# One queue in source order for the transfers of the first three products of an encoder block

## Chip, cores and metric

The kernel runs on one core of a Trainium2 chip. The metric is the device time of one execution in microseconds (us). PE is TensorE, DVE VectorE, ACT ScalarE, POOL GpSimd, SP the engine that issues most transfers.

## What is computed

One encoder block for 256 tokens `x` and 256 memory tokens `mem` of width 2048, all in float32. Cut to what matters here:

```python
h = rms_norm(x, g_mix);  proj = h @ w_in          # q, k, v of mixers A, B; q of C; three gates
mkv = rms_norm(mem, g_mem) @ w_mem_kv             # k and v of mixer C: the first two products
kc = rms_norm(split_heads(mkv[..., :C_W]), g_kc)  # each head normed again with its gains
# A: dilated windows with a bias; B: grouped queries with rotary; C: cross-attention into mem
x = x + (sum of gates * branch @ w_br) @ w_o
hf = rms_norm(x, g_ffn) @ w_ffn_in
x = x + (silu(hf[..., :D_FF]) * hf[..., D_FF:]) @ w_ffn_out
```

The row scale of an RMS norm (one number for each token) is applied behind the product, and the gains `g` in front of it, on the transposed tokens.

## The kernel before, in words

**A product.** `product` (line 150) multiplies 256 tokens by a weight of 2048 x 512 (4.19 MB): 16 blocks k of 128 rows. A block has six matmuls of 128x128 by 128x512: for each half t of the tokens, high x high, high x low and low x high (lines 172 to 174), since every operand is split into a high and a low part in TensorE's float32r. The two halves go to two PSUM banks from a pool of four (`pmm`), so every second product writes the same banks again and needs them evacuated.

**Splits.** `split` (line 72) makes the high part on ACT (line 75, or 78 with gains) and the remainder on DVE (76, 79). Weights go from `raw` (three buffers, two blocks of 512 KB in each load of the first two products, four blocks in the third) to `whi` and `wlo` (four buffers of two blocks). `load_T` (179) does the same for the transposed tokens, 256 KB for two blocks: its `get(k)` issues the transfer to `rawT` (two buffers) on ACT's queue (190) when block k is first asked for, and splits it right after.

**Order.** The first three products are `w_mem[0]` (keys of mem), `w_mem[1]` (values of mem) and `w_qkv[0]`. Beside them generators run as side jobs: `product` calls `tick` (129) after each block, and a tick advances at most one job whose pause, counted in blocks, is over. `row_sums` (198) loads 512 KB of token rows on SP, pauses, squares them on ACT with a running sum (206), four times, and then makes the row scale on DVE. `take_slots` (289) evacuates a product: squares of the banks (298), a pause, a wait for the row scale, the head scale `hf` (309), a pause, then the scaled copy `y` out of the banks (313), the gains and the rotary on POOL, the transposes of heads `hT` on PE. `constants` (241) loads head gains `gh`, the rotary table and a bias table on SP; `fetch` (249) asks for the blocks of xT ahead.

This order in the source isn't the order on the engines. The program is handed to a planner, which simulates the engines and their transfers and picks, for each engine, among the instructions that are ready in its simulation the one that is earliest in the source. The order that it finds is fixed: on the chip each engine runs its list in order and waits at an instruction whose data has not come. `s4` tiles (rows, `y`, squares, rotary) share five buffers of 4 KB in each partition.

Of the kernel before, what the change touches and what calls it, by code (L numbers as in the profile page):

```python
# [11 lines left out]
F32 = mybir.dt.float32  # L12
F32R = mybir.dt.float32r
I32 = mybir.dt.int32
AF = mybir.ActivationFunctionType
# [3 lines left out]
P = 128  # L19
S = 256  # L20
T = S // P
D = 2048
KT = D // P
HD = 128
DFF = 5632
NC = 512
KF = DFF // P
PK, LOAD = 2, 4
# [8 lines left out]
BUCKETS, MAX_DIST = 32, 1024  # L37
# [13 lines left out]
def encoder_block(ctx: ExitStack, tc: tile.TileContext, a: dict, out: bass.AP):  # L51
    nc = tc.nc
    const = ctx.enter_context(tc.tile_pool(name="const", bufs=1))
    wp = ctx.enter_context(tc.tile_pool(name="wp", bufs=3))
    big = ctx.enter_context(tc.tile_pool(name="big", bufs=11))
    mid = ctx.enter_context(tc.tile_pool(name="mid", bufs=5))
    small = ctx.enter_context(tc.tile_pool(name="small", bufs=4))
    dram = ctx.enter_context(tc.tile_pool(name="dram", bufs=1, space=bass.MemoryType.DRAM))
    pmm = ctx.enter_context(tc.tile_pool(name="pmm", bufs=4, space=bass.MemoryType.PSUM))
# [2 lines left out]
    def s8(shape, name, dt=F32R, pool=None):  # L62
        return (pool or big).tile(shape, dt, name=name, tag="s8")

    def s4(shape, name, dt=F32):
        return mid.tile(shape, dt, name=name, tag="s4")

    def at_bank(name):
        return pat.tile([P, NC], F32, name=name, tag="at")


    def split(hi, lo, src, scale=None):

        if scale is None:
            nc.scalar.activation(hi, src, AF.Copy)  # L75
            nc.vector.tensor_sub(lo, src, hi.bitcast(F32))  # L76
        else:
            nc.scalar.activation(hi, src, AF.Copy, scale=scale)
            nc.vector.scalar_tensor_tensor(lo, src, scale, hi.bitcast(F32), op0=ALU.mult, op1=ALU.subtract)
# [22 lines left out]
    def row_scale(ss, r):  # L102

        v = small.tile([P, T], F32, name="rs_v")
        nc.vector.tensor_scalar(v, ss, 1.0 / D, EPS, op0=ALU.mult, op1=ALU.add)
        y = rsqrt(v, [P, T], nc.vector)
        nc.vector.tensor_copy(r[:, 0], y)
        nc.vector.tensor_mul(r[:, 1], y, y)


    side, now = [], [0]

    def advance(job):

        try:
            lag = next(job[1])
            job[0] = now[0] + (lag or 1)
            return lag is not None
        except StopIteration:
            side.remove(job)  # L120
            return True

    def start(steps):

        job = [0, steps]
        side.append(job)
        advance(job)

    def tick():
        now[0] += 1  # L130
        for job in list(side):
            if job[0] <= now[0] and advance(job):
                break
# [5 lines left out]
    def load(src, k0, nk):  # L139

        raw = wp.tile([P, LOAD, NC], F32, name="raw")
        if nk % PK:
            c = k0 % PK * NC
            nc.sync.dma_start(out=raw[:, 0], in_=src[k0 // PK][:, c:c + NC])
        else:
            nc.sync.dma_start(out=raw[:, :nk].rearrange("p (u k) n -> p u (k n)", k=PK),
                              in_=src[k0 // PK:(k0 + nk) // PK].rearrange("u p n -> p u n"))
        return raw

    def product(src, lhs, nk, head=(), beside={}):  # L150


        ps = [pmm.tile([P, NC], F32, name="mm") for _ in range(T)]
        k0 = 0
        while k0 < nk:
            n = head[0] if head else min(LOAD, nk - k0)
            head = head[1:]
            if k0 in beside:
                start(beside[k0])
            lhs(k0)  # L160
            raw = load(src, k0, n)
            for b in range(0, n, PK):
                m = min(PK, n - b)
                hi = wp.tile([P, PK, NC], F32R, name="whi", bufs=4)
                lo = wp.tile([P, PK, NC], F32R, name="wlo", bufs=4)
                split(hi[:, :m], lo[:, :m], raw[:, b:b + m])
                for i in range(m):
                    k = k0 + b + i
                    xh, xl = lhs(k)
                    for t in range(T):  # L170
                        c = slice(t * P, (t + 1) * P)
                        nc.tensor.matmul(ps[t], lhsT=xh[:, c], rhs=hi[:, i], start=(k == 0), stop=False)  # L172
                        nc.tensor.matmul(ps[t], lhsT=xh[:, c], rhs=lo[:, i], start=False, stop=False)  # L173
                        nc.tensor.matmul(ps[t], lhsT=xl[:, c], rhs=hi[:, i], start=False, stop=(k == nk - 1))  # L174
                    tick()
            k0 += n
        return ps

    def load_T(src, g, tag):

        tiles = [s8([P, 4, 2, S], tag) for _ in range(KT // 4)]
        have = set()

        def get(k):
            k0 = k // 2 * 2
            tl = tiles[k // 4]
            if k0 not in have:
                have.add(k0)
                raw = wp.tile([P, 2, S], F32, name="rawT", bufs=2)
                nc.scalar.dma_start(out=raw, in_=src[k0 // 2].rearrange("p (k s) -> p k s", s=S))  # L190
                for i in range(k0, k0 + 2):
                    split(tl[:, i % 4, 0], tl[:, i % 4, 1], raw[:, i - k0], g[:, i:i + 1])
            return tl[:, k % 4, 0], tl[:, k % 4, 1]
        return get

# [2 lines left out]
    def row_sums(src, r, pace, name):  # L198

        ss = small.tile([P, T, 2], F32, name="rss", bufs=1)  # L200
        for t in range(T):
            for h in range(2):
                rows = s4([P, D // 2], "rows")
                nc.sync.dma_start(out=rows, in_=src[t * P:(t + 1) * P, h * (D // 2):(h + 1) * (D // 2)])
                yield pace
                nc.scalar.activation(rows, rows, AF.Square, accum_out=ss[:, t, h:h + 1])  # L206
        sr = small.tile([P, T], F32, name="ss", bufs=1)
        nc.vector.tensor_reduce(sr, ss, axis=AX.X, op=ALU.add)
        row_scale(sr, r)
        known.add(name)  # L210

    def transposed(src, dst, g=None):

        for h in range(2):
            tp = at_bank("tp")
            for k in range(2):
                for t in range(T):
                    nc.tensor.transpose(tp[:, k * S + t * P:k * S + (t + 1) * P],  # L218
                                        src[t][:, (2 * h + k) * P:(2 * h + k + 1) * P], ident)
            if g is None:  # L220
                d = dst(2 * h, 2)
                split(d[0], d[1], tp.rearrange("p (k s) -> p k s", s=S))
            else:
                for k in range(2):
                    d = dst(2 * h + k, 1)
                    split(d[0], d[1], tp[:, k * S:(k + 1) * S], g(2 * h + k))
# [10 lines left out]
    gh = const.tile([P, 6, HD], F32, name="gh")  # L237
    rope = const.tile([P, 2, T, HD // 2], F32, name="rope")
    relb = const.tile([P, A_HEADS], F32, name="relb")

    def constants():
        v = a["g_heads"]
        nc.sync.dma_start(out=gh, in_=bass.AP(tensor=v.tensor, offset=v.offset, ap=[[0, P], [HD, 6], [1, HD]]))
        yield 1
        nc.sync.dma_start(out=rope, in_=a["rope"])
        nc.vector.memset(relb[:64], NEG)
        nc.sync.dma_start(out=relb[:BUCKETS], in_=a["rel_bias"])

    def fetch(get, pace):
        for k in range(0, KT, 2):  # L250
            get(k)
            yield pace
# [174 lines left out]
    r_m, r_x, r_f = (scales[:, i] for i in range(3))  # L427
    memT = load_T(a["memT"], gT[:, 1], "memT")
    xT = load_T(a["xT"], gT[:, 0], "xT")
    memT(0)  # L430
    first = product(a["w_mem"][0], memT, KT, (1, 1) + (2,) * 7, {6: row_sums(a["mem"], r_m, 3, "mem")})
    start(constants())
    start(take_slots(first, MEM_SLOTS[:4], r_m, "mem", nc.vector))
    start(fetch(xT, 2))
    start(take_slots(product(a["w_mem"][1], memT, KT, (2,) * 8), MEM_SLOTS[4:], r_m, "mem"))
    oT = [s8([P, 4, 2, S], f"oT{i}") for i in range(3)]
    ol = lambda k: (oT[k // 4][:, k % 4, 0], oT[k // 4][:, k % 4, 1])
    for c in range(8):
        sums = {} if c else {0: row_sums(a["x"], r_x, 3, "x")}
        start(take_slots(product(a["w_qkv"][c], xT, KT, beside=sums), SLOTS[4 * c:4 * c + 4], r_x))  # L440
        if c == 0:
            start(biases())
# [28 lines left out]
    x = [s8([P, D], f"x{t}", F32) for t in range(T)]  # L471
# [20 lines left out]
    for c0, c1 in ((0, 6), (6, KF // 4)):  # L492
        hT = []
        for n in range(c0, c1):
            ap = product(a["w_ffn_a"][n], x1l, KT)
# [7 lines left out]
            tl = s8([P, 2, 4, S], "hT", pool=tail if n % 6 < 4 and n < 6 or n > 8 else None)  # L503
# [91 lines left out]
```

## Time and profile before

| | us |
|---|---|
| median of 3 runs | 1437.49 (1437.03 to 1438.25) |
| profiled run, its own time | 1438.22 |
| its span | 1436.4 |
| PE busy | 1416.7 (99%) |
| DVE busy | 781.2 (54%) |
| ACT busy | 667.2 (46%) |
| POOL busy | 78.8 (5%) |
| transfers, mean | 193 GB/s |

How to read it: a busy PE is not PE at its peak, since matmuls overlap; what one matmul costs is seen in the distance between two starts. TensorE's clock has two levels, 1.2 and 2.4 GHz, shown as a granted share of 0.5 or 1.0. In rows of time the first number is the start in us from the start of the span, the second the duration; brackets hold the idle time of the engine before the instruction and what ended it. ACTq and SPq are issues of transfers by these engines.

### The profile page before, as it was taken

To read this page: it belongs to the slowest core of one execution; us is meant where nothing else is said; L and a number is where in the kernel's file an instruction comes from. 1 tells how busy PE (TensorE), PEld (TensorE's weight loads), DVE (VectorE), ACT (ScalarE), POOL (GpSimd) and SP (SyncE) were. 2 spreads that over 40 slices of the span, in tenths; PEclk is the share of its full clock that TensorE was granted. 3 is DMA by queue.
4 is the path that set the end of the run, shared out by engine and by line. 5 is a ranking of instruction groups with operands and counts; after the bars stand their busy time and mean duration, and the time that the engine had idled before them with its cause. 6 is when DMAs were issued, how large, how long until landed. Compare 5 with 4: busy or idle time off the path is not lost.

```text
span 1436.4 us, 16231 instructions
## 1 busy us (share of the span) xinstructions
PE 1416.7 (99%) x6422; PEld 1170.0 (81%) x6422; DVE 781.2 (54%) x912; ACT 667.2 (46%) x860; POOL 78.8 (5%) x146
## 2 busy tenths in 40 slices
PE   6999999999999999999999999999999999999998
PEld 4778788888888888888888888888888888888887
DVE  5677766744555555555644555545444445554543
ACT  6676555644444444444444444444333444444432
POOL 0013642200000000000000000000000000000000
PEclk9999999999999999999999999999999999999999
DMA  8876445465555556555555555565555555556562
GB/s 294 282 248 204 147 153 173 160 222 197 196 192 194 176 189 213 184 187 177 183 197 186 194 177 204 176 205 177 203 179 203 187 194 179 202 177 204 192 218 88
DMA packets 75772, 276.98 MB, mean 193 GB/s; under 512 B 5232, under 2 KB 7792, under 8 KB 75440
## 3 DMA queue, kind: packets, MB, share of 16 engines
q1 hardware_dynamic: 73248, 271.73, 56.0%
q10 hardware_dynamic: 2448, 4.22, 0.8%
q8 instruction: 50, 0.82, 0.2%
q14 instruction: 26, 0.21, 0.0%
HBM read 273.05 MB, written 2.88 MB: 192 GB/s over the span
## 4 chain that ended last, share of the span: by engine, by line
PE 92%; DMA 3%; POOL 2%; ACT 1%; issue 1%; DVE 1%; SPq 0%; ACTq 0%; DVEq 0%; POOLq 0%
PE mm L173 29%; PE mm L172 29%; PE mm L174 29%; PE tp L218 1%; DMA rawT<-in_xT 1%; DMA rows<-in_x 1%; DMA rows<-in_mem 1%; POOL rot L337 1%; POOL rot L340 1%; POOL rtmp L338 1%; ACT whi L75 0%; PE pT L396 0%; ACT rows L206 0%; PE hT L346 0%; POOL y L320 0%
## 5 line engine op out<-in xcount | busy, mean ns | idle before, releaser
L76 DVE TENSOR_TENSOR wlo<-raw,whi 128x1024 fp32r<-128x1024 f32 (+1 forms) x497 | 614.7, 1239 | 584.9 <-ACT whi L75 582.6
L75 ACT ACTIVATE whi<-raw 128x1024 fp32r<-128x1024 f32 (+1 forms) x497 | 525.5, 1061 | 642.6 <-PE mm L174 616.6
L174 PE MATMUL mm<-whi,x1T 128*128 128x512 f32 x704 | 274.8, 390 | 0.0
L172 PE MATMUL mm<-whi,x1T 128*128 128x512 f32 x704 | 274.8, 390 | 0.0
L173 PE MATMUL mm<-wlo,x1T 128*128 128x512 f32 x704 | 274.1, 389 | 0.0
L173 PE MATMUL mm<-wlo,xT 128*128 128x512 f32 x640 | 250.2, 391 | 1.0 <-DVE wlo L76 1.0
L172 PE MATMUL mm<-whi,xT 128*128 128x512 f32 x640 | 250.5, 392 | 0.1
L174 PE MATMUL mm<-whi,xT 128*128 128x512 f32 x640 | 249.5, 391 | 0.0
L173 PEld LDWEIGHTS mm<-wlo,x1T 128*128 128x128 f32 x704 | 132.2, 188 | 27.2
L174 PEld LDWEIGHTS mm<-whi,x1T 128*128 128x128 f32 x704 | 132.2, 188 | 27.1
L172 PEld LDWEIGHTS mm<-whi,x1T 128*128 128x128 f32 x704 | 132.2, 188 | 26.9
L173 PEld LDWEIGHTS mm<-wlo,xT 128*128 128x128 f32 x640 | 120.2, 188 | 26.1 <-DVE wlo L76 1.4
L172 PEld LDWEIGHTS mm<-whi,xT 128*128 128x128 f32 x640 | 120.1, 188 | 25.3 <-issue 0.8
L174 PEld LDWEIGHTS mm<-whi,xT 128*128 128x128 f32 x640 | 120.2, 188 | 24.4
L173 PE MATMUL mm<-wlo,hT 128*128 128x512 f32 x352 | 137.8, 391 | 0.0
L172 PE MATMUL mm<-whi,hT 128*128 128x512 f32 x352 | 137.7, 391 | 0.0
L174 PE MATMUL mm<-whi,hT 128*128 128x512 f32 x352 | 137.0, 389 | 0.0
L172 PEld LDWEIGHTS mm<-whi,hT 128*128 128x128 f32 x352 | 66.1, 188 | 14.4
L174 PEld LDWEIGHTS mm<-whi,hT 128*128 128x128 f32 x352 | 66.1, 188 | 14.3
L173 PEld LDWEIGHTS mm<-wlo,hT 128*128 128x128 f32 x352 | 66.1, 188 | 13.5
L173 PE MATMUL mm<-wlo,mT 128*128 128x512 f32 x128 | 50.8, 397 | 0.0
L172 PE MATMUL mm<-whi,mT 128*128 128x512 f32 x128 | 50.5, 395 | 0.0
(123 smaller groups left out, 997.5 us busy)
## 6 DMA issues: line engine op xcount, KB each, us to landing
raw<-in_w_gate SPq DMA_DIRECT2D x48, 1024.0 KB, 5.0
raw<-in_w_ffn_a SPq DMA_DIRECT2D x44, 1024.0 KB, 5.0
raw<-in_w_ffn_b SPq DMA_DIRECT2D x44, 1024.0 KB, 5.0
raw<-in_w_ffn_out SPq DMA_DIRECT2D x44, 1024.0 KB, 5.0
raw<-in_w_qkv SPq DMA_DIRECT2D x32, 1024.0 KB, 5.1
raw<-in_w_o SPq DMA_DIRECT2D x16, 1024.0 KB, 5.0
raw<-in_w_br SPq DMA_DIRECT2D x8, 1024.0 KB, 4.9
raw<-in_w_mem SPq DMA_DIRECT2D x15, 512.0 KB, 4.9
```

The lines of the kernel that those rows point to most:

```text
L75: nc.scalar.activation(hi, src, AF.Copy)
L76: nc.vector.tensor_sub(lo, src, hi.bitcast(F32))
L172: nc.tensor.matmul(ps[t], lhsT=xh[:, c], rhs=hi[:, i], start=(k == 0), stop=False)
L173: nc.tensor.matmul(ps[t], lhsT=xh[:, c], rhs=lo[:, i], start=False, stop=False)
L174: nc.tensor.matmul(ps[t], lhsT=xl[:, c], rhs=hi[:, i], start=False, stop=(k == nk - 1))
L218: nc.tensor.transpose(tp[:, k * S + t * P:k * S + (t + 1) * P], src[t][:, (2 * h + k) * P:(2 * h + k + 1) * P], ident)
L337: nc.gpsimd.tensor_mul(ov[:, :, :, c], xv[:, :, :, c], cs[0])
L338: nc.gpsimd.tensor_mul(tmp[:, :n], xv[:, :, :, 1 - c], cs[1])
L340: op(ov[:, :, :, c], ov[:, :, :, c], tmp[:, :n])
```

## The change

Five edits, which act on the first three products only, that is while fewer than 48 ticks have passed.

- `ordered` puts an edge without a semaphore from an instruction to the last one traced before it on the same engine, so that the planner can't issue it earlier than that. It is put on all SP issues of weights, tokens, rows and tables, and on the squares of token rows.
- The pieces of memT and xT go out on SP instead of ACT, four blocks (two transfers of 256 KB) into one `s4` tile. `get(k, True)` only issues; a new side job `ahead` does so four blocks at a time: memT from block 1, one tile every 3 ticks; xT from the end of the first product, every 4 ticks. The `s4` pool has six buffers instead of five, and the two `rawT` buffers are gone.
- In `product` the load of the weights stands ahead of the split of the tokens.
- `row_sums` of mem starts at block 8 instead of 6, both with a pace of 4 instead of 3; each square stands behind the next load of rows.
- `constants` pauses 8 ticks instead of 1 between its tables, `fetch` 4 before it begins.

```diff
+    def ordered(ins):
+        return tc.keep_in_program_order(ins) if now[0] < 3 * KT else ins
...
-    mid = ctx.enter_context(tc.tile_pool(name="mid", bufs=5))
+    mid = ctx.enter_context(tc.tile_pool(name="mid", bufs=6))
...
-            lhs(k0)
             raw = load(src, k0, n)
+            lhs(k0)
...
-        def get(k):
+        def get(k, fetch=False):
+            k0, q = k // 2 * 2, k // 4
+            tl = tiles[q]
+            if q not in raws:
+                raw = raws[q] = s4([P, 4, S], "rawT")
+                for u in range(2):
+                    ordered(nc.sync.dma_start(out=raw[:, 2 * u:2 * u + 2],
+                                              in_=src[2 * q + u].rearrange("p (k s) -> p k s", s=S)))
+            if fetch:
+                return
             if k0 not in have:
                 have.add(k0)
-                raw = wp.tile([P, 2, S], F32, name="rawT", bufs=2)
-                nc.scalar.dma_start(out=raw, in_=src[k0 // 2].rearrange("p (k s) -> p k s", s=S))
...
+        for i in range(len(parts) + 1):
+            if i < len(parts):
+                t, h = parts[i]
+                rows.append(s4([P, D // 2], "rows"))
+                ordered(nc.sync.dma_start(out=rows[i],
+                                          in_=src[t * P:(t + 1) * P, h * (D // 2):(h + 1) * (D // 2)]))
+            if i:
+                t, h = parts[i - 1]
+                ordered(nc.scalar.activation(rows[i - 1], rows[i - 1], AF.Square, accum_out=ss[:, t, h:h + 1]))
+            yield pace
...
-    memT(0)
-    first = product(a["w_mem"][0], memT, KT, (1, 1) + (2,) * 7, {6: row_sums(a["mem"], r_m, 3, "mem")})
+    memT(0, True)
+    first = product(a["w_mem"][0], memT, KT, (1, 1) + (2,) * 7, {1: [ahead(memT, 3, 4)], 8: [row_sums(a["mem"], r_m, 4, "mem")]})
     start(constants())
     start(take_slots(first, MEM_SLOTS[:4], r_m, "mem", nc.vector))
+    start(ahead(xT, 4))
     start(fetch(xT, 2))
```

## Rows read from the trace of the kernel before

**Rows 1.** The page, part 1: busy time of each engine.
```profile
PE 1416.7 (99%) x6422; PEld 1170.0 (81%) x6422; DVE 781.2 (54%) x912; ACT 667.2 (46%) x860; POOL 78.8 (5%) x146
```

**Rows 2.** Waits of PE, whole span: who waited for whom, total us, times, longest.
```profile
PE mm L172 <- ACT memT L78: 11.9, 2, 6.2
PE hT L346 <- POOL rot L340: 1.7, 2, 1.4
PE mm L173 <- DVE wlo L76: 1.0, 1, 1.0
```

**Rows 3.** Timeline of PE, first two products and the start of the third.
```profile
6.16 0.79 PE L172 MATMUL mm<-whi,memT 128*128 128x512 f32 x1 [6.16 <-ACT memT L78]
6.75 0.63 PE L173 MATMUL mm<-wlo,memT 128*128 128x512 f32 x1
7.18 0.63 PE L172 MATMUL mm<-whi,memT 128*128 128x512 f32 x1
...
13.36 0.61 PE L174 MATMUL mm<-whi,memT 128*128 128x512 f32 x2
19.75 0.80 PE L172 MATMUL mm<-whi,memT 128*128 128x512 f32 x1 [5.77 <-ACT memT L78]
...
61.36 0.39 PE L174 MATMUL mm<-whi,memT 128*128 128x512 f32 x1
61.58 0.39 PE L172 MATMUL mm<-whi,xT 128*128 128x512 f32 x1
```

**Rows 4.** Timeline of ACT, 13 to 24 us.
```profile
14.17 1.06 ACT L206 ACTIVATE rows<-rows 128x1024 f32<-128x1024 f32 x1 [3.33 <-DMA rows<-in_mem]
...
17.30 1.99 ACT L75 ACTIVATE whi<-raw 128x1024 fp32r<-128x1024 f32 x2
19.20 0.90 ACT L78 ACTIVATE memT<-rawT,gT 128x256 fp32r<-128x256 f32 x2
22.50 0.33 ACTq L190 DMA_DIRECT2D rawT<-in_memT  x1
22.93 1.06 ACT L75 ACTIVATE whi<-raw 128x1024 fp32r<-128x1024 f32 x1 [2.84 <-DVE rs_y L93]
```

**Rows 5.** Timeline of SP, the issues up to 24 us.
```profile
0.73 0.87 SPq L144 DMA_DIRECT2D raw<-in_w_mem  x2
...
2.12 3.04 SPq L204 DMA_DIRECT2D rows<-in_mem  x4
5.30 1.48 SPq L146 DMA_DIRECT2D raw<-in_w_mem  x2
...
12.07 9.62 SPq L146 DMA_DIRECT2D raw<-in_w_mem  x3
```

**Rows 6.** Stretches: length, busy PE, PEld, DVE, ACT, POOL; clock; DMA share; GB/s.
```profile
8.00:13.00 5.00, 5.00 (x18) 3.96 (x17) 2.02 (x3) 2.72 (x5) 0.00 (x0) 1.00 1.00 392
...
16.00:18.00 2.00, 0.00 (x0) 0.00 (x0) 0.50 (x3) 2.00 (x5) 0.00 (x0) 0.86 1.04 387
...
18.00:24.00 6.00, 4.02 (x9) 2.75 (x10) 4.76 (x18) 3.16 (x6) 0.00 (x0) 0.50 0.57 187
...
39.80:61.60 21.80, 21.80 (x98) 18.03 (x97) 17.06 (x36) 15.27 (x29) 0.00 (x0) 1.00 0.83 267
```

**Rows 7.** Issues of transfers, 0 to 40 us: count, size, median us to landing.
```profile
rawT<-in_memT ACTq DMA_DIRECT2D x8, 256.0 KB, 4.3
rows<-in_mem SPq DMA_DIRECT2D x4, 512.0 KB, 8.0
```

**Rows 8.** Timelines of ACT and DVE: evacuation of the first product.
```profile
45.25 0.58 ACT L298 ACTIVATE sq<-mm 128x512 f32<-128x512 f32 x1
...
57.45 0.17 DVE L309 TENSOR_TENSOR hf<-rs_y,scales 128x8 f32<-128x8 f32 x1
...
60.88 1.40 ACT L313 ACTIVATE y<-mm,hf 128x128 f32<-128x128 f32 x5
```

**Rows 9.** Waits of SP's queue up to 80 us, columns as in rows 2.
```profile
SPq L146 <- DVE wlo L76: 26.5, 12, 5.7
```

More of the change, by code (lines that the diff above doesn't have):

```diff
@@ L143, in load @@
             c = k0 % PK * NC
-            nc.sync.dma_start(out=raw[:, 0], in_=src[k0 // PK][:, c:c + NC])
+            ordered(nc.sync.dma_start(out=raw[:, 0], in_=src[k0 // PK][:, c:c + NC]))
         else:
-            nc.sync.dma_start(out=raw[:, :nk].rearrange("p (u k) n -> p u (k n)", k=PK),
-                              in_=src[k0 // PK:(k0 + nk) // PK].rearrange("u p n -> p u n"))
+            ordered(nc.sync.dma_start(out=raw[:, :nk].rearrange("p (u k) n -> p u (k n)", k=PK),
+                                      in_=src[k0 // PK:(k0 + nk) // PK].rearrange("u p n -> p u n")))
         return raw
@@ L157, in product @@
             head = head[1:]
-            if k0 in beside:
-                start(beside[k0])
+            for job in beside.get(k0, ()):
+                start(job)
+            raw = load(src, k0, n)
             lhs(k0)
-            raw = load(src, k0, n)
             for b in range(0, n, PK):
@@ L181, in load_T @@
         tiles = [s8([P, 4, 2, S], tag) for _ in range(KT // 4)]
-        have = set()
-        def get(k):
-            k0 = k // 2 * 2
-            tl = tiles[k // 4]
+        raws, have = {}, set()
+        def get(k, fetch=False):
[8 more added lines that the diff above has]
+                return
             if k0 not in have:
                 have.add(k0)
-                raw = wp.tile([P, 2, S], F32, name="rawT", bufs=2)
-                nc.scalar.dma_start(out=raw, in_=src[k0 // 2].rearrange("p (k s) -> p k s", s=S))
                 for i in range(k0, k0 + 2):
-                    split(tl[:, i % 4, 0], tl[:, i % 4, 1], raw[:, i - k0], g[:, i:i + 1])
+                    split(tl[:, i % 4, 0], tl[:, i % 4, 1], raws[q][:, i % 4], g[:, i:i + 1])
             return tl[:, k % 4, 0], tl[:, k % 4, 1]
@@ L200, in row_sums @@
         ss = small.tile([P, T, 2], F32, name="rss", bufs=1)
[L201 to L206, printed above, removed]
+        parts = [(t, h) for t in range(T) for h in range(2)]
+        rows = []
+        for i in range(len(parts) + 1):
[8 more added lines that the diff above has]
+            yield pace
         sr = small.tile([P, T], F32, name="ss", bufs=1)
@@ L242, in constants @@
         v = a["g_heads"]
-        nc.sync.dma_start(out=gh, in_=bass.AP(tensor=v.tensor, offset=v.offset, ap=[[0, P], [HD, 6], [1, HD]]))
-        yield 1
-        nc.sync.dma_start(out=rope, in_=a["rope"])
+        ordered(nc.sync.dma_start(out=gh, in_=bass.AP(tensor=v.tensor, offset=v.offset, ap=[[0, P], [HD, 6], [1, HD]])))
+        yield 8
+        ordered(nc.sync.dma_start(out=rope, in_=a["rope"]))
         nc.vector.memset(relb[:64], NEG)
-        nc.sync.dma_start(out=relb[:BUCKETS], in_=a["rel_bias"])
+        ordered(nc.sync.dma_start(out=relb[:BUCKETS], in_=a["rel_bias"]))
     def fetch(get, pace):
+        yield 4
         for k in range(0, KT, 2):
@@ L429, in encoder_block, with ahead @@
     xT = load_T(a["xT"], gT[:, 0], "xT")
-    memT(0)
-    first = product(a["w_mem"][0], memT, KT, (1, 1) + (2,) * 7, {6: row_sums(a["mem"], r_m, 3, "mem")})
+    def ahead(get, pace, k0=0):
+        for k in range(k0, KT, 4):
+            get(k, True)
+            yield pace
+    memT(0, True)
+    first = product(a["w_mem"][0], memT, KT, (1, 1) + (2,) * 7, {1: [ahead(memT, 3, 4)], 8: [row_sums(a["mem"], r_m, 4, "mem")]})
     start(constants())
     start(take_slots(first, MEM_SLOTS[:4], r_m, "mem", nc.vector))
+    start(ahead(xT, 4))
     start(fetch(xT, 2))
@@ L438, in encoder_block @@
     for c in range(8):
-        sums = {} if c else {0: row_sums(a["x"], r_x, 3, "x")}
+        sums = {} if c else {0: [row_sums(a["x"], r_x, 4, "x")]}
         start(take_slots(product(a["w_qkv"][c], xT, KT, beside=sums), SLOTS[4 * c:4 * c + 4], r_x))
```

## The prediction

> **What bounds the kernel now.** I read the page first: TensorE (PE) is busy for 1416.7 of 1436.4 us [rows 1], so a change that takes no matmul away can win only what PE loses. The waits of PE say where that is: 11.9 us in two waits for splits of memT, and 2.7 for the rest [rows 2]. PE's timeline gives both waits their place: 6.16 us before the first matmul, and 5.77 us that end at 19.75 [rows 3].
>
> The loss is best counted in k-blocks of six matmuls. The third product begins at 61.58 (the first matmul on xT), when two products, 2 x 16 x 6 = 192 matmuls, are done [rows 3]. At full rate a matmul starts 0.22 to 0.23 us after the last (61.36 to 61.58; 0.227 over longer stretches), so 192 take 43.5 us; they took 61.58 - 6.16 = 55.4. The 11.9 us too many fall into four parts:
> - the first ten matmuls start 0.43 us apart (6.75 to 7.18) instead of 0.227, and the first takes 0.59: about 2.2 us;
> - a hole after block 3: the last two matmuls start at 13.36, so PE is done with them at 13.36 + 2 x 0.227 = 13.8, and the next starts at 19.75: 5.9 us;
> - after the hole PE is at half rate again, granted clock 0.50 (1.2 instead of 2.4 GHz) from 18 to 24 [rows 6]: nine matmuls at 0.2 us too many, and 0.5 of a slow start and one wait: 2.3 us. PE had stood still since 13.8 when the clock fell (the mean of 0.86 in 16 to 18 puts that at about 17.4);
> - the rest, 1.5 us, is in scattered waits up to 35 us, each under 0.6.
>
> Then the cause of the hole. ACT's timeline [rows 4]: at 14.17 it ends a wait of 3.33 us for token rows of mem, does three squares of them up to 17.3, then the weight splits, and at 19.20 the memT split that PE needs. ACT works in order, so the weights of block 4 stand behind squares that nobody needs yet. SP's queue [rows 5] says why the rows were late and the weights with them: four row transfers of 512 KB go out at 2.12, ahead of the weights of blocks 4 to 7 (5.30). Rows take a median of 8.0 us to land [rows 7].
>
> A second such place is on ACT at 22.50 [rows 4]: the issue of a memT transfer, which waits for one of two rawT buffers, stands in ACT's own stream, and the weight split behind it ends an idle time of 2.84 us. It costs PE part of the scattered 1.5 us.
>
> **What the change does to this.** *Rows and squares later.* In the source the rows of mem move from block 6 to block 8 and then come every 4 blocks; each square is pinned behind a weight split whose load was issued after those rows. All SP issues of the three products are pinned to source order, so the four rows can't go out at 2.12 again. The hole (5.9) and the second half-rate stretch (2.3) go: -8.2 us. What is late next is the load of the blocks themselves. One block is 262 KB of weights and 131 KB of memT, 0.39 MB in 1.36 us of PE, 289 GB/s; with a backlog the engines move 392 GB/s (8 to 13 us) [rows 6]. For the first product with its two rows, 4.19 + 2.10 + 1.05 = 7.3 MB, that is 18.7 us at 392, beside 24 us of PE. For the second, 4.19 + 2.10 of xT + 1.05 of rows + 0.39 of head gains + 0.13 of rope = 7.9 MB, 20.1 us beside 21.8. The third, 4.19 + 1.57 = 5.8 MB, has room. So transfers stay just ahead, without much to spare: an issue that waits for a buffer lets the engines run dry. I put +1.0 us for new small waits in the first two products; bounds 0 (backlog all along) and +4.0 (three queued loads of 0.52 MB at 392 GB/s, 1.34 us each, ahead of a needed piece).
>
> *memT and xT pieces from ACT's queue to SP's.* 16 issues of 0.33 us [rows 4] leave ACT, 5.3 us, and go to SP. SP waits for the split that frees a raw buffer, 26.5 us in 12 waits up to 80 us [rows 9], which hides them. Behind each of those waits now stand the pieces of memT and xT too. The wait of 2.84 us on ACT goes, since the pieces have the four-block buffers of the mid pool (6 instead of 5, each 4 KB per partition) and no issue on ACT: I take half of the scattered losses, -0.8; bounds -1.5 and 0.
>
> *The start.* Two memT issues go ahead of the first weights on SP, but the memT split comes ahead of the weight split. The two issues cost at most 0.9 (two issues take 0.87 at 0.73 [rows 5]); the split of memT, the last thing that PE waited for, then comes ahead of a weight split on ACT and gains at most 0.7. I take 0.
>
> *Row scales later.* With rows every 4 blocks the scale of mem is known in the source at tick 28 instead of 18 (I walked the ticks, one job per tick), and the evacuation of the first product (y) comes at tick 32 instead of 22. The third product writes the same two PSUM banks from tick 32 on. Today that evacuation has no margin: its last y starts in the group of five at 60.88 and ends at 62.28 [rows 8], where PE reaches the second bank at about 62.26. But what made it late was not the scale. The squares of mem were over at 17.3; the squares of the product's own banks came at 45.25, and VectorE's chain from there to hf ended at 57.45. So 28 us lay between the scale's inputs and their use; 10 ticks of 1.36 us eat 13.6 of them. I take 0; bounds 0 and +13.6 plus 2.3 for the clock. The scale of x goes from tick 45 to 58, y of the first qkv product from 54 to 62, wanted at 64. There the last two squares are no longer pinned; cost 0, same bound.
>
> *Left as they are:* 1.0 us for a late weight remainder in the third product, and 1.7 us in two waits of head transposes for GpSimd's rotary products [rows 2]. Bounds for both: -2.7 and, if the planner's new order makes the longer one twice what it is, +1.4.
>
> **Sum.** -8.2 + 1.0 - 0.8 = -8.0 us. The profiled run took 1438.22 us around a span of 1436.4; that is 0.7 above the median 1437.49. By it the changed kernel takes 1430.2, against the median 1429.5. Best end of all terms: -8.2 - 1.5 - 0.7 - 2.7, some -13, about 1425.
>
> **A rule against it.** Today the pieces of memT overtake: they land in 4.3 us where rows take 8.0 [rows 7], from a queue of their own. The Trainium skill, "DMA: Bandwidth & Descriptors", section on queues, rings and completion order, says that each DMA engine takes turns between queues that have work, packet by packet; on one queue that turn is lost and a piece waits for all that was issued before it. The trace agrees in that overtaking. By that rule alone the change would be rival 2. The same page's specifications put HBM for one core at some 358 GB/s; by it the second product's 7.9 MB would take 22.1 us, an estimate, 0.3 longer than PE. The 392 GB/s of [rows 6] speak against that limit here.
>
> **Rivals.** *1, slower: late scales.* If y of the first product really moves by the 10 ticks of the source, PE stands 13.6 us at the start of the third product, and its clock falls as in the hole, 2.3: -8.0 + 15.9 = +7.9, 1445.4 us. It decides from a stand of 10.9 us there (8.0 won and 2.9 for 0.2%). For it: no margin today, and the squares are pinned behind splits that wait for PE. Against: the 28 us above, and a product that now ends 8 us earlier, so that its squares and the scale come at the same time. Chance 0.12.
>
> *2, pieces wait in the one queue.* No piece overtakes; at the two or three places where a pinned row or piece stands behind loads that wait for a raw buffer, PE loses up to 4.0 us instead of 1.0, and 1.0 more at the next: -4.0, 1433.5 us (1431 to 1437). For it: SP's 26.5 us of waits [rows 9]. Against: in source order a piece goes out two to six blocks ahead of its use. Chance 0.15.
>
> *3, the change doesn't do what it says.* Pins hold rows and squares; the splits of xT and memT are free, and the planner may put them on ACT before their data has landed, as it did with the squares. A new stand of 2.8 to 3.3 us on ACT [rows 4] with its 2.3 of clock: -2.5, 1435.0. Against: from 39.8 to 61.6 PE was busy throughout, with ACT idle for three tenths of it [rows 6]. Chance 0.08.
>
> **How the numbers follow.** Forecast 0.62, 1429.5 us, its own range 1425.5 to 1433; rival 1 0.12; rival 2 0.15; rival 3 0.08; still faster (the 2.7 us of [rows 2] go too) 0.03. A range of 1425 to 1437 leaves out rival 1 and little else. A measurement of this kernel can tell 0.2%, 2.9 us, from no change: under 1434.6 is faster. The forecast, the 0.03, and about two thirds of rivals 2 and 3 lie there, kept a little lower for causes not listed: 0.76. Same 0.11, slower 0.13.
>
> **What would show it.** Right: PE's wait for memT shrinks to the first one, near 6 us; no idle time over 1 us between 7 and 30; one half-rate stretch, with the granted clock at 1.0 from about 11 us on; the first xT matmul at 53.5 instead of 61.58; the four mem rows issued between about 8 and 32 us; no transfer issue on ACT but that of the gains. Wrong by rival 1: a wait of the third product's first matmul for ACT's y. By rival 2: PE waits for weights or for splits whose raw or rawT landed late, with DMA not busy. By rival 3: ACT idle before a split, released by a DMA, and PE idle right after. The later waits of [rows 2] may move by one or two us either way without any of these.

## The result, and the profile after

The changed kernel takes 1443.0 us (median of 7 runs, 1442.48 to 1445.15), the kernel before beside it 1438.15: a ratio of 1.0037 [1.0025, 1.0049]. It is slower by 0.3 to 0.5%, where 1429.5 us was forecast and 1437 was the upper end of the range. The profiled run took 1442.77 us around a span of 1441.0, which is 4.6 more than before. The rest of this section finds these 4.6 us, and the 8 us that were to be won.

The waits of PE (columns as in [rows 2]):

```profile
PE mm L176 <- ACT whi L79: 9.8, 3, 6.3
PE hT L363 <- POOL y L337: 2.8, 1, 2.8
PE hT L363 <- POOL rot L357: 1.4, 2, 0.9
PE mm L177 <- DVE wlo L80: 1.0, 2, 0.5
```

The first wait of 6.3 us is the start, as before. The 5.77 us of [rows 3] are gone, but PE now waits 3.2 us for a weight split and 2.8 us for GpSimd's y, which it didn't do in [rows 2]. The timeline of PE puts them in place:

```profile
6.28 1.22 PE L176 MATMUL mm<-whi,memT 128*128 128x512 f32 x2 [6.28 <-ACT whi L79]
...
15.09 0.62 PE L176 MATMUL mm<-whi,memT 128*128 128x512 f32 x2
...
35.97 0.93 PE L176 MATMUL mm<-whi,memT 128*128 128x512 f32 x2 [3.23 <-ACT whi L79]
...
62.91 1.30 PE L363 MATMUL hT<-ident,y 128*128 128x128 f32 x8 [2.83 <-POOL y L337]
64.59 2.07 PE L287 MATMUL bias_ps<-oneh,rep 64*128 64x512 f32 x2 [0.38 <-DVE headT L80]
66.60 1.22 PE L176 MATMUL mm<-whi,xT 128*128 128x512 f32 x2
```

Block 4 now starts at 15.09 instead of 19.75. The first xT matmul starts at 66.60 instead of 61.58, and 53.5 was forecast. 192 matmuls at 0.227 us take 43.5; 66.60 - 6.28 = 60.3, so 16.8 us are lost on the way instead of 11.9. Counted block by block from the starts of every fourth block: 3.4 in blocks 0 to 3 (matmuls start 0.43 us apart until 12.2), 1.2 in blocks 4 to 11, 3.4 in blocks 12 to 15, 2.2 in blocks 16 to 19, nothing in 20 to 27, 6.7 from block 28 to the third product. So there are two new holes, each with a stretch at half rate behind it (columns as in [rows 6]):

```profile
36.00:38.00 2.00, 1.50 (x4) 0.77 (x5) 2.00 (x3) 2.00 (x4) 0.00 (x0) 0.59 0.05 17
...
64.00:71.00 7.00, 6.62 (x14) 4.01 (x14) 6.54 (x12) 4.94 (x9) 0.00 (x0) 0.54 0.30 83
```

The granted clock is 0.59 and 0.54 in them. The second lasts to about 70.5 and takes 1.9 us more from the third product's first two blocks. Part of what stands ahead of 66.60 is not lost: the eight head transposes and two bias matmuls at 62.91 to 66.60 lay later in the kernel before. That is why the 5.0 us of lag at 66.60 don't grow by those 1.9: by the third product's last block it is 4.4, at the end of the span 4.6.

**The first hole** (block 16, the first of the second product) has two causes. SP's queue from 16 us on, and the weights' time to landing (min/median/max, in the view of the tile raw, 24 to 36 us):

```profile
16.86 5.47 SPq L150 DMA_DIRECT2D raw<-in_w_mem  x2
22.38 0.42 SPq L217 DMA_DIRECT2D rows<-in_mem  x1
22.86 0.42 SPq L259 DMA_DIRECT2D gh<-in_g_heads  x1
23.32 0.93 SPq L195 DMA_DIRECT2D rawT<-in_xT  x2
24.35 1.79 SPq L150 DMA_DIRECT2D raw<-in_w_mem  x2
```
```profile
DMA to landing us min/median/max: 7.1/8.2/8.5
```

SP waits 5.5 us for a raw buffer. What had come due meanwhile goes out in one go, in source order: a row transfer, the head gains and two pieces of xT, 1.4 MB, all ahead of the weights of block 16. Those go out at 24.35 and land 7.1 us later, at 31.5. And ACT, which could split them then, has another order:

```profile
32.11 1.28 ACT L315 ACTIVATE sq<-mm 128x512 f32<-128x512 f32 x2 [4.29 <-PE mm L178]
33.28 1.69 ACT L82 ACTIVATE xT<-rawT,gT 128x256 fp32r<-128x256 f32 x4
34.88 1.99 ACT L79 ACTIVATE whi<-raw 128x1024 fp32r<-128x1024 f32 x2
```

ACT stands 4.29 us at the squares of the first product's banks, which need its last matmuls, then makes four splits of xT that nobody needs before the third product, and only then, at 34.88, the weight split that PE wants, 3.4 us after its weights had landed. Had the split, 1.06 us for one load, come first, it would have been done at 32.6, when PE was done with the first product: in this run the hole is ACT's order, and the late landing would have cost next to nothing by itself.

**The second hole** is the late scale of mem. ACT and DVE:

```profile
41.78 1.04 ACT L221 ACTIVATE rows<-rows 128x1024 f32<-128x1024 f32 x1
...
58.26 2.17 ACT L330 ACTIVATE y<-mm,hf 128x128 f32<-128x128 f32 x8 [4.86 <-DVE hf L326]
```
```profile
44.46 0.29 DVE L284 COPY rep<-relb 64x64 f32<-64x64 f32 x2 [1.33 <-DMA relb<-in_rel_bias]
44.67 0.14 DVE L224 TENSOR_REDUCE ss<-rss 128x2 f32<-128x4 f32 x1
...
46.56 0.16 DVE L90 TENSOR_SCALAR rs_y<-rs_h 128x2 int32<-128x2 int32 x1
46.63 1.27 DVE L83 SCALAR_TENSOR_TENSOR xT<-rawT,gT,xT 128x256 fp32r<-128x256 f32 x3
47.81 0.15 DVE L95 SCALAR_TENSOR_TENSOR rs_t<-rs_y 128x2 f32<-128x2 f32 x1
...
55.23 0.15 DVE L112 TENSOR_TENSOR scales<-rs_y 128x2 f32<-128x2 f32 x1
...
58.05 0.17 DVE L326 TENSOR_TENSOR hf<-rs_y,scales 128x8 f32<-128x8 f32 x1
```

The fourth square of mem's rows runs at 41.78 (in the kernel before all four were over at 17.3, [rows 4]), though its rows, issued at 26.19, had landed after 9.1 us, at 35.3: it is pinned behind a weight split. It is over at 42.9, but DVE's list has a copy of the bias table ahead of the sum, and DVE stands 1.33 us for that table, which the change moved behind a pause of 8 ticks. The sum follows at 44.67, and then the scale takes 10.6 us to 55.23, because between its steps of 0.15 us DVE's list holds splits of 1.2 us. hf is there at 58.05, ACT has waited 4.86 us for it, y goes to GpSimd, and PE, whose list has the head transposes of y ahead of the third product, waits until 62.91.

The Trainium skill, "DMA: Bandwidth & Descriptors", section on queues, rings and completion order, was weighed in the prediction: each DMA engine takes turns between the queues that have work, so a piece that leaves its own queue loses its turns between the loads of the other. The trace after agrees in direction: up to 40 us a piece of memT lands after a median of 4.9 us instead of the 4.3 of [rows 7]. That is 0.6 us, and no wait of PE in the profile names a piece; what the one queue is seen to cost is the pile at 22.38, with ACT's order that goes with it, not the turns.

### The profile page after: what moved, and what is told of

The parts are those of the page before. It is cut to its first block, busy times and chain, and to the rows that moved or that the text cites. A ratio compares the mean times of both kernels' runs of the same rounds, so it can differ in the third digit from the quotient of the medians.

```text
span 1441.0 us, 16231 instructions
## 1 busy us (share of the span) xinstructions
PE 1420.3 (99%) x6422; PEld 1171.0 (81%) x6422; DVE 781.7 (54%) x912; ACT 668.2 (46%) x860; POOL 75.9 (5%) x146
## 4 chain that ended last, share of the span: by engine, by line
PE 92%; DVE 3%; DMA 2%; ACT 1%; POOL 1%; issue 1%; SPq 0%; DVEq 0%; ACTq 0%; POOLq 0%
PE mm L177 30%; PE mm L176 30%; PE mm L178 30%; DMA raw<-in_w_mem 2%; PE tp L234 1%; DVE wlo L80 1%; ACT whi L79 1%; ACT y L330 1%; PE pT L413 0%; DVE pr L403 0%; POOL rtmp L355 0%; PE hT L363 0%; POOL rot L357 0%; POOL rot L354 0%; PE bias_ps L287 0%
## 5 line engine op out<-in xcount | busy, mean ns | idle before, releaser
L177 PEld LDWEIGHTS mm<-wlo,x1T 128*128 128x128 f32 x704 | 132.2, 188 | 27.2
L178 PEld LDWEIGHTS mm<-whi,x1T 128*128 128x128 f32 x704 | 132.2, 188 | 27.2
```

## The experiments

Each kernel is the changed one with the edit shown, unless it says otherwise; times are medians, ratios are to the kernel before, run beside it.

**1. The scale of mem known from the start.** The scale in the result is 1, known from the start; the rows are still loaded, squared and summed.

```diff
+    nc.gpsimd.memset(r_m, 1.0)
+    known.add("mem")
-    ... {8: [row_sums(a["mem"], r_m, 4, "mem")]}
+    ... {8: [row_sums(a["mem"], r_d, 4, "mem")]}
```

> The changed kernel with the same transfers and squares, but the first two products use a row scale of mem that is set to one at the start; what the squares give goes to a tile that nobody reads. So the output for mixer C is not the reference's. Late-scale theory: ACT no longer waits for the head scale between 53.4 and 58.3 us, the third product begins at 59 to 60 us instead of 66.6, there is no half-rate stretch there, and the time falls by 5 to 7 us, to 1436 to 1438. Rival, the third product waits for its weights in the one queue (they land at 57.3 and 59.9): the third product begins at 63 or later and less than 3 us are won. The hole at 32 to 36 us stays in both.

1437.22 us, 0.9991 [0.9982, 1.0001], 5.8 us less than the changed kernel. y starts at 40.5 instead of 58.26, and the first xT matmul at 64.08 directly follows the second product's last. So the late scale is what made the second hole. The expectation had the third product at 59 to 60: there the second product loses more than in the changed kernel (4.5 us in blocks 16 to 27 instead of 2.2, with the eight head transposes now among them and a wait of 1.64 us for a remainder at 38.18). The first hole stays:

```profile
PE mm L176 <- ACT whi L79: 9.9, 4, 6.0
PE mm L177 <- DVE wlo L80: 2.9, 4, 1.6
```

**2. The first hole by its two causes.** First ACT's order: the squares of the product's banks come 3 ticks later in the source.

```diff
+            if name == "mem":
+                yield 3
             for t in range(T):
                 src = ps[t][:, :n * HD]
```

> The changed kernel, with the squares of the first product's banks 3 ticks later in the source, so that ACT has a weight split of the second product ahead of them. Theory that ACT's order makes the hole at 32.6 to 36.0 us: PE's idle time there falls from 3.4 us to about 1 (the weights land at 31.5, then 1.1 for the split and up to 1.2 for its remainder), no half-rate stretch follows, and 2 to 5 us are won by the end of the first product, if nothing behind it takes them back. Rival, late transfers alone: the hole stays over 2.5 us. The stand at the third product stays in both, and may take back what was won, since the row scale is bound to the queue and not to PE.

1441.18 us, 1.0021 [1.0012, 1.0031]. Block 16 starts at 32.75 instead of 35.97. Of these 3.2 us 1.7 come from before: the first product's last matmul starts at 30.67 instead of 32.36, mostly since its blocks 4 to 11 lose 0.1 us instead of 1.2 in the planner's new order. The hole itself shrinks from 3.4 to 1.9 us. ACT now goes to the weight split as soon as the weights land, and what is left of the hole is the transfer, measured against a product that ends earlier (timelines of ACT and PE):

```profile
31.64 1.06 ACT L79 ACTIVATE whi<-raw 128x1024 fp32r<-128x1024 f32 x1 [0.33 <-DMA raw<-in_w_mem]
```
```profile
32.75 0.73 PE L176 MATMUL mm<-whi,memT 128*128 128x512 f32 x2 [1.68 <-ACT whi L79]
```

Then the transfers: the head gains wait 6 ticks, the first piece of xT 2, so that they go out behind the weights.

```diff
     def constants():
         v = a["g_heads"]
+        yield 6
...
     def ahead(get, pace, k0=0):
+        if k0 == 0:
+            yield 2
```

> The changed kernel, with the head gains 6 ticks later and the first pieces of xT 2 ticks later, so that the second product's first weights stand on SP behind one row transfer instead of 1.4 MB. Transfer theory of the hole at 32.6 us: the weights land about 2.3 us earlier (0.9 MB at 400 GB/s), near 29, and the hole goes wholly, with 3.4 us and 2.2 of half rate. ACT-order theory: if the squares of the banks still stand ahead of the first weight split, the hole stays at about 2 us, whenever the weights land. The third product still waits for the late row scale in both.

1441.01 us, 1.0017 [1.0007, 1.0026]. Block 16 starts at 32.14 without a wait; one of 0.51 us stands two blocks later, at 35.53. So the hole goes wholly, as the transfer theory had it, but ACT's order has changed too: the planner now puts block 16's split ahead of the squares, which start at 31.66 (timeline of ACT).

```profile
28.65 1.06 ACT L79 ACTIVATE whi<-raw 128x1024 fp32r<-128x1024 f32 x1 [0.72 <-DMA raw<-in_w_mem]
```

The two causes are not independent, then: with weights that land early, the squares no longer stand in the way. Each of the two edits brings block 16 forward by more than 3 us, and behind each the second hole is longer, by 2.7 and 2.8 us; the waits of PE in the second (spread; 5.5 in sq_later):

```profile
PE mm L176 <- ACT whi L79: 7.3, 2, 6.7
PE hT L364 <- POOL y L338: 5.7, 1, 5.7
```

The third product starts at 65.35 (sq_later) and 65.40 (spread), against 66.60. It goes by y, and y hardly moves (56.84 in spread): the sum of mem comes 4.9 us earlier there, at 39.77, but the scale then takes 14.1 us on DVE, to 53.83.

**3. The scale off DVE.** Its Newton steps go to GpSimd.

```diff
-        y = rsqrt(v, [P, T], nc.vector)
+        y = rsqrt(v, [P, T], eng)
...
-        row_scale(sr, r)
+        row_scale(sr, r, nc.gpsimd if name == "mem" else nc.vector)
```

> The changed kernel with the three Newton steps of the row scale of mem on GpSimd, which is idle then, instead of on VectorE: 12 short operations. In the changed kernel the chain from the sum of squares (44.7) to the scale (55.2) takes 10.6 us on VectorE, between weight remainders and xT splits, where before it took 5.5. Chain theory: the scale is there 4 to 6 us earlier, y starts at 53 to 55 instead of 58.3, and the stand at the third product shrinks from 6.7 us (59.9 to 66.6) by 3 to 5, to 1438 to 1440. Rival, the late squares alone: y starts less than 2 us earlier and the time stays over 1441.

1439.42 us, 1.0011 [1.0002, 1.002]. From the sum to the scale it is 7.6 us instead of 10.6 (42.48 to 50.1), hf comes at 55.28 instead of 58.05, and of the wait of 2.8 us for y 0.4 is left. But little of that is the chain. The steps from the scale to hf are still on DVE, and they now take 5.2 us instead of 2.8, with splits between them: from the sum to hf it is 12.8 us instead of 13.4. The sum itself comes 2.2 us earlier, and this run is 1.4 us ahead at block 4 already (13.73 instead of 15.09), which the edit doesn't explain. And PE, no longer kept by y, waits 1.61 us for a weight split at the third product's first matmul (62.89). So the expectation's time was met, its theory was not shown: moving a part of the chain moved the splits into the next part, and how much of the lateness DVE's alternation carries stays open.

**4. The rows of mem early, by the source** (from block 2, every 3 blocks).

```diff
-    ... {8: [row_sums(a["mem"], r_m, 4, "mem")]}
+    ... {2: [row_sums(a["mem"], r_m, 3, "mem")]}
```

> The changed kernel, with the rows of mem from block 2 on and 3 ticks apart instead of from block 8 and 4 apart; the scale is then known in the source at tick 17 instead of 28. Late-scale theory: the stand at the third product goes, 4 to 7 us won there. Transfer theory: two more row transfers, 1.05 MB or 2.6 us at 400 GB/s, stand ahead of weights of the first product, so PE waits 2 to 5 us more before 30 us, and the sum comes near 1438 to 1442.

1443.97 us, 1.0037 [1.0023, 1.0051]: no gain. The stand at the third product is gone (y at 44.6), but row transfers go ahead of the first product's blocks again: PE waits 1.63 us before 12.70 and runs at half rate from 13.96 to 17.10, the hole at block 16 stays at 3.4, and two later waits of 2.6 and 2.9 us (before 140.3 and 175.3 us) take what is left.

**5. The pins.** All taken off (`ordered` gives back its instruction, the queue and the pace stay), and, in the kernel before, put on alone (pieces stay on ACT's queue with two buffers).

```diff
     def ordered(ins):
-        return tc.keep_in_program_order(ins) if now[0] < 3 * KT else ins
+        return ins
```

> The changed kernel with its edges taken out (the pieces of memT and xT stay on SP, all pauses stay), so the planner may order SP's issues and the squares freely again. If the edges are what moves the rows out of the way: the four rows go out before 10 us, three squares stand on ACT ahead of weight splits, and the hole of before comes back, 5 to 6 us before 22 us with its half-rate stretch of 2. If the pauses alone did it, no hole over 1 us stands before 30. In either case the row scale is known earlier than in the changed kernel, so the stand at the third product is under 3 us. Time: 1438 to 1444.

> The kernel before with the edges alone, on SP's issues and on the squares of the first three products; memT and xT stay on ACT's queue, rows start at block 6 with a pace of 3, and no pause is changed. Theory that the loss of the changed kernel lies in the late row scale and in the transfers ahead of the second product: neither is here (scale at tick 18, pieces on a queue of their own), so the hole at 14 goes and nothing takes its place; the third product begins at 53 to 56 us and the time is 1429 to 1434. Rival, the edges themselves cost: weights wait behind rows in order, the first product has waits of 3 us and more, and the time is 1436 or higher.

Without pins 1442.43 us, 1.0031 [1.0019, 1.0043]; I had expected no stand over 3 us at the third product, and there is one of 6.07, by ACT's y itself (timeline of PE):

```profile
63.77 0.80 PE L176 MATMUL mm<-whi,xT 128*128 128x512 f32 x1 [6.07 <-ACT y L330]
```

Three of the four rows go out at 7.8 to 9.4, and PE waits 1.78 us before 19.63, with a half-rate stretch to 24.4 behind it: blocks 4 to 7 lose 5.3 us, less than the 8.2 of the kernel before, and neither of the two theories fits. But the fourth goes out only at 34.92, behind nine loads of weights and two pieces of xT. So the scale is late without the pins too; whether the fourth rows waited for their place in the source or for a buffer of the pool that they now share with the pieces wasn't told apart. The pins alone are worst, 1449.42 us, 1.0083 [1.0064, 1.0102], where I had expected a gain. Here the scale is known at 38, and y is late by ACT's own waits:

```profile
48.46 1.06 ACT L78 ACTIVATE whi<-raw 128x1024 fp32r<-128x1024 f32 x1
55.54 0.91 ACT L81 ACTIVATE xT<-rawT,gT 128x256 fp32r<-128x256 f32 x2 [6.02 <-DMA rawT<-in_xT]
...
63.85 0.91 ACT L81 ACTIVATE xT<-rawT,gT 128x256 fp32r<-128x256 f32 x2 [5.45 <-DMA rawT<-in_xT]
64.67 2.15 ACT L316 ACTIVATE y<-mm,hf 128x128 f32<-128x128 f32 x8
```

PE waits 10.7 us for y ahead of its head transposes. A piece of xT that ACT issues at 48.00 is split at 55.54; DVE's remainders behind it wait too, with the steps to hf among them (43.21 to 60.11), and y stands behind the second of these waits. So the pins without the pieces fetched ahead into larger buffers cost 11 us here. That fetching ahead is what makes them bearable is argued from these waits; the kernel before also has other pauses than the changed one, and that was not separated.

**6. Both causes at once.** The spread of experiment 2, with the rows of mem from block 6 every 3 blocks, as in the kernel before; and that pace alone.

```diff
-    ... {8: [row_sums(a["mem"], r_m, 4, "mem")]}
+    ... {6: [row_sums(a["mem"], r_m, 3, "mem")]}
```

> The changed kernel with the head gains 6 ticks and the first xT pieces 2 ticks later, and the rows of mem from block 6 on with a pace of 3, as before the change; the scale is then known in the source at tick 21 instead of 28. Late-scale theory: the evacuation y is over before the second product ends, the third product begins within 1 us of it, at 54 to 57 us, and the time is 1431 to 1435. Rival, the scale's chain on VectorE is slow wherever it stands (10.6 us in the changed kernel): y still ends after 55 us and the stand stays over 3 us, 1437 or more.

> The changed kernel with one edit: the rows of mem begin at block 6 instead of 8 and come every 3 blocks instead of 4 (as in the kernel before); the tables and the first piece of xT stay where the change puts them. With the transfers at tick 16 spread as well, the same edit gave 1431.8 us (0.996 [0.9945, 0.9975] of the kernel before). Theory (two separate losses, each of which brings the other back where it alone is mended): the stand at the start of the third product goes (y of the first product by 48 us, third product's first matmul right behind the second's last), the hole at block 16 stays (2.5 to 4.5 us of wait for ACT's weight split, with a half-rate stretch behind it): 1435 to 1439 us. Rival (the pace of the rows alone was the cause, and the spreading of the tables added nothing): 1431 to 1433 us, with no wait of over 2 us at block 16.

Together 1431.8 us, 0.996 [0.9945, 0.9975]: 11.2 us less than the changed kernel, 6 less than the one before. The pace alone takes 1439.81 us, 1.001 [1.0001, 1.0019]. In the first, PE loses nothing over 0.25 us at any place from 11.9 to 46.7, the scale runs from 28.55 to 36.61 (8.1 us), y starts at 44.01, and the third product at 56.62 (stretches; timelines of ACT and PE):

```profile
14.00:30.00 16.00, 16.00 (x73) 13.18 (x72) 9.99 (x15) 12.95 (x19) 0.00 (x0) 1.00 0.98 364
30.00:36.00 6.00, 6.00 (x28) 4.99 (x27) 5.71 (x14) 4.82 (x9) 0.00 (x0) 1.00 1.00 355
36.00:46.00 10.00, 10.00 (x46) 8.29 (x45) 7.57 (x26) 5.85 (x15) 0.00 (x0) 1.00 0.86 295
```
```profile
44.01 2.17 ACT L331 ACTIVATE y<-mm,hf 128x128 f32<-128x128 f32 x8 [2.91 <-DVE hf L327]
```
```profile
48.68 1.09 PE L364 MATMUL hT<-ident,y 128*128 128x128 f32 x8 [1.57 <-POOL y L338]
51.49 0.50 PE L177 MATMUL mm<-wlo,memT 128*128 128x512 f32 x1 [1.25 <-DVE wlo L80]
```

With the pace alone the first hole stays, as the theory had it, and costs twice: the clock falls behind it (0.74 from 36 to 46), and y at 50.16 (by 48 was expected) stands ahead of weight splits on ACT, so that its late hf holds up the second product.

```profile
35.36 1.22 PE L176 MATMUL mm<-whi,memT 128*128 128x512 f32 x2 [3.22 <-ACT whi L79]
54.82 1.97 PE L363 MATMUL hT<-ident,y 128*128 128x128 f32 x8 [2.56 <-POOL y L337]
```

Eleven us from the two edits, where spread alone gave 2.0 and the pace alone 3.2. The fourth square of mem's rows shows how the losses hang together (timelines of ACT, the pace alone and both):

```profile
35.21 1.04 ACT L221 ACTIVATE rows<-rows 128x1024 f32<-128x1024 f32 x1
```
```profile
27.28 1.04 ACT L221 ACTIVATE rows<-rows 128x1024 f32<-128x1024 f32 x1
```

With the pace alone its rows, issued at 21.65, land after 6.7 us, at 28.4; but the square stands in ACT's list behind block 16's weight split (34.26), so the first hole itself makes the scale late. With both it is over before that split.

**7. Is there a third cost?** Spread together with the free scale of experiment 1, and the fastest version with its scale on GpSimd as in experiment 3.

> The changed kernel with both causes taken away: the table of head gains and the first piece of xT wait behind the first weights of the second product (6 and 2 ticks later), and the scale of mem is left out of the result: it is set to 1 at the start, while its rows are still loaded, squared and summed into a scale that nobody uses. Theory (the two together are the whole of what the change lost against the forecast of 1429.5 us): no wait of PE over 2 us in the first 70 us but that for the first weights, one stretch at half rate, at the start, the third product's first matmul by 57 us: 1428 to 1432 us. Rival (a third cost, of transfers on the one queue or of the rows' place, remains): over 1433 us, with waits for splits of memT or weights whose transfers landed late.

> The fastest version so far (transfers of tick 16 spread, rows of mem from block 6 every 3 blocks: 1431.8 us) with one more edit: the five-step scale of mem is worked out on GpSimd instead of VectorE, where its short operations alternate with weight and xT splits of 1.2 us (8.0 us from the sum to the scale there). Theory (VectorE's alternation costs PE something even where the scale is early, since the short operations also push splits back): the wait of 1.73 us for y at 46.7 and the wait of 1.42 us for a split at 49.9 shrink by half or more, 1429 to 1431 us. Rival (the scale has room now, and GpSimd's own short operations are slower): within 1 us of 1431.8.

The first takes 1435.89 us, 0.9982 [0.9973, 0.9992], and its theory fell: 1428 to 1432 was expected. With the scale known, y and hf are early in the planner's lists as well: DVE does the steps to hf ahead of a weight remainder, PE waits 1.65 us for it before 37.77, and the third product starts at 58.88, 2.3 us later than in the fastest version; behind it GpSimd's rotary products are waited for 3.2 us instead of 1.9. A chain of short steps costs PE something when it is early, too. But of the 2.3 us 1.4 stand at block 16 already (32.00 instead of 30.63): blocks 4 to 11 lose 1.9 us here and nothing in the fastest version, with a wait of 0.74 us before 20.16 for a split whose weights ACT had waited 2.65 us for. That is the sign of the rival, a small third cost of the transfers with the rows at the changed kernel's pace. The second takes 1432.21 us, 0.9959 [0.9944, 0.9974]: no different from 1431.8, as its rival had it. Once the scale has room, the engine that works it out doesn't matter.

## Why the prediction was wrong, point by point

- **The hole and the second half-rate stretch, -8.2: right in kind, some 7 of it arrived.** Rows no longer go out at 2.12, ACT no longer stands for them, and block 12 starts at 27.15 instead of 33.96. The start is 1.2 us worse than before: matmuls start 0.43 us apart until 12.2 instead of 10.6, with a wait of 0.26 us at 9.47 that wasn't there; why isn't shown, and the granted clock reads 1.00 from 7 to 12.5. So 6.8 us had been won by 27 us, and all of it, and 5.0 more, was lost by 66.60.
- **New small waits in the first two products, +1.0 (0 to +4.0): the term was mis-sized.** It measured 5.6 in blocks 12 to 19. The 1.4 MB that stand pinned ahead of the second product's first weights were in the sum, but as bytes spread over the product; 20.1 us of transfers in 21.8 of PE say nothing about which comes first. And the term looked at transfers alone: ACT's order, squares and xT splits ahead of the weight split, kept landed weights waiting for 3.4 us. Rival 2 came nearest, with rows and pieces pinned ahead of loads and a price of 4.0; ACT's order was in none of the cases.
- **ACT's 2.84 us stand, -0.8: right in kind, its size not told apart.** No piece is issued on ACT. Blocks 4 to 11 lose 1.2 us, where 1.5 were scattered up to 35 us; what the stand gave back and what new small waits took there is one number.
- **Row scales later, +0 (0 to +13.6 and 2.3): this is the step that failed,** and rival 1, at a chance of 0.12, had the mechanism. The reason given against it was a slack of 28 us between the scale's inputs and their use. But the slack was counted to squares of the banks at 45.25 and a y at 60.88 that were late for reasons of their own. Without the hole the second product ends 8 us earlier and wants y 8 us earlier; this had been seen, but the scale doesn't come "at the same time". And the shift was counted from source to source, 10 ticks or 13.6 us. In the kernel before the squares didn't run at their place in the source: the planner had let them overtake, and they were over at 17.3. The pins take that away for all four (without them three overtake again, and the fourth runs at 41.70, experiment 5). The last square is over at 42.9, 25.6 us later; the sum, behind the wait for the bias table, comes 27.2 us later (44.67 instead of 17.43), and its steps, 5.4 us long in the trace before, take 10.6 where splits stand between them (8.1 to 14.1 in other versions). Together that is 32.4 us, more than the slack of 28. Experiment 6 shows the price of the source order: with spread, y starts at 44.01 instead of 56.84 when the sum of mem stands 7 ticks earlier in the source. The sum comes 11.2 us earlier (28.55 instead of 39.77), the scale on DVE takes 8.1 instead of 14.1, and the steps from it to hf take 7.2 instead of 2.8: 12.8 in all. The stand itself was smaller than 13.6: 2.8 us in the changed kernel, whose first hole had made PE late as well, and 5.5 to 6.1 where the first hole was smaller.
- **The sign of what would be seen** held for rival 1 with a difference: not the third product's first matmul waits for ACT's y, but head transposes that the planner had put ahead of it wait for GpSimd's y (2.34 us more). In the version without pins it is the matmul itself, 6.07 us.
- **Left as they are, 0:** the waits for GpSimd's rotary products take 1.4 us instead of 1.7. The wait for a late remainder in the third product is gone; that PE's row for remainders again says 1.0 is luck, these are two others, 0.52 before 22.03 and 0.50 before 37.40.
- **Rival 3** (splits put on ACT before their data has landed) did not occur as such: at the first hole ACT's idle time ended by PE, at the second by DVE.

What stays open: why the planner puts the squares of the banks and four xT splits ahead of the weight split of block 16. Its simulated times are not in the trace; that it does so, that it doesn't with the transfers spread, and what it costs, is shown, the reason isn't. Nor was it settled which of the two edits of experiment 6 gives how much, since neither gives much alone.

## What to carry to other kernels

When a hole early in the kernel closes, everything behind it is wanted earlier: for each step that the change also delays in the source, count its slack against the new, earlier need, and not against the time at which it was used before. Ask also where an instruction really ran before: a pin takes it back to its place in the source, and from an overtaking place that is further than the lines that you moved. Two late inputs hide each other, and one can make the other late: mending either gave 2 to 3 us of 11 here, so look, before you judge an edit by its time, whether the other wait grew by as much. And in a queue that is pinned to source order the question is not whether the bytes fit, but which bytes stand ahead of the first ones that are wanted after each wait for a buffer.

## What the runs showed of the hardware

A chain of dependent steps of 0.15 us on an in-order engine takes as long as what its list holds between them: the same scale of mem took 5.4 us before the change, 8.1, 10.6 and 14.1 in three versions of it on DVE, and 7.6 with its Newton steps on GpSimd, whose list is empty there. DVE and GpSimd also take longer beside each other: four xT splits take 1.66 us at 34.55 in the changed kernel, and 3.49 in the fastest version at 46.61, while GpSimd works on y (46.27 to 48.63); one of GpSimd's steps takes 1.04 us instead of 0.19 beside a DVE split at 31.96 (spread_rows63_pool). That the one causes the other was not tested. The transfers reached 417 GB/s over 4 us, just ahead of the first hole (a stretch of the changed kernel):

```profile
28.00:32.00 4.00, 4.00 (x19) 3.30 (x19) 0.04 (x1) 0.00 (x0) 0.00 (x0) 1.00 1.05 417
```

That is above the 358 GB/s that the Trainium skill's page "DMA: Bandwidth & Descriptors" (specifications) gives as the limit of HBM for one core, half of what a stack has for two. By it the second product's loads would have been longer than its matmuls; the measurement decides.
